# Weight blocks of the first attention split by two GpSimd transfers each, and its keys as split products

## The chip, the cores and the metric

The kernel runs on one core of a Trainium2 chip. The metric is the device time of one execution in microseconds (us). Its engines run side by side, each through its own list of instructions in order: TensorE (PE in the profile; its weight loads are PEld), VectorE (DVE), ScalarE (ACT), GpSimd (POOL) and SyncE (SP, which here only issues transfers). An instruction whose input isn't ready holds up all that stand behind it on its engine.

## The reference

Two transformer blocks follow each other on 256 tokens of width 1024, in fp32. The change lies in the first block's attention:

```python
u = rms_norm(h, pre_mix_gain[l])
proj = u @ w_in[l]
qa, ka, va, qb, kb, vb, g = jnp.split(proj, SPLITS, axis=-1)
qa = rope(...); ka = rope(...); qb = rope(...); kb = rope(...)
o_swa = windowed_gqa_sink_attention(qa, ka, va, attn_sink[l], pos, is_real)
o_diff = differential_attention(qb, kb, vb, lam, lambda_init, diff_subln_gain[l], is_key)
gates = jax.nn.sigmoid(g + b_gate[l])
```

`h` is the tokens behind 16 meta tokens, 272 columns that count. `o_swa` has 16 query and 4 key heads of 64, `o_diff` 8 heads that each subtract one softmax from another. Everything after it (branch products, output product, a gated feed-forward, and the whole second block) is as before in both kernels.

## The kernel before

All activations lie transposed, features on the partitions, tokens along the row. A weight matrix is stored in blocks of 128 output columns: one block is a 128x1024 fp32 tile (512 KB), which holds 8 squares of 128x128, one for each 128 input features.

A product of a block with the activations is made in one of two ways. `gemm_whole` (line 341) multiplies the fp32 block with fp32 activations, 8 products. `gemm` (line 325) works on numbers that are split into a high part of type fp32r and a low part, the remainder: high weight x high activation, high weight x low activation, low weight x high activation, 24 products, the 16 with the high weights first. The activations are split once (`uh`, `ul`), the weights block by block in `load_w`: SP loads the block into one of three `raw` buffers (line 299), ScalarE writes the high part `wh` as a copy in fp32r (line 309), VectorE the low part `wl = raw - wh` (line 311); `wh` and `wl` have three buffers each. (`wshare` is 0 throughout, so that the subtraction is always VectorE's.)

The first attention's projections are 52 blocks: 8 for the queries (`w_qb`), 8 for the keys (`w_kb`) and 8 for the values (`w_vb`) of the differential heads, 8 for the queries of the windowed heads (`w_qa`), 4 for their keys and values (`w_kva`), 16 for the gates (`w_gate1`). The 8 of `w_kb` and the first 2 of `w_kva`, the keys, go through `gemm_whole`; the other 42 through `gemm`. The first two blocks of all, one of keys and one of values, are loaded ahead of everything (`wfirst`). The keys and queries are then rotated (`rope`): ScalarE copies the product out of PSUM, VectorE shuffles it, GpSimd multiplies and adds (lines 511 to 513), and ScalarE and VectorE split the result.

Sixteen attention units (one differential head, or two windowed heads) stand in the order `ORDER`; the projections of a unit are written two units ahead of its attention, the gates' blocks between the units. A scheduler turns this into one list per engine; the lists are fixed when the program is built. Behind the units come 8 blocks of the differential branch (`branch_d`, `w_bd`), and from there on every block is split in the same way.

## Time and profile before

| | us |
|---|---|
| three timed runs, median (lowest to highest) | 992.06 (989.26 to 992.2) |
| the profiled execution's own time | 991.08 |
| its span, first to last instruction | 988.8 |

| engine | busy us | share of the span |
|---|---|---|
| TensorE, products | 967.2 | 98% |
| TensorE, weight loads | 902.1 | 91% |
| VectorE | 686.8 | 69% |
| ScalarE | 545.3 | 55% |
| GpSimd | 223.4 | 23% |

The shares are over the whole program; the first attention is its first quarter, so its own shares have to be asked for by the stretch. Products of TensorE are pipelined: the duration of one overlaps the next, and how long a run of them takes is read from their starts. An fp32 product appears as two instructions in the trace, a split one as one.

### The profile page before, as it was taken

Reading aid. Unit: us, or ns where it says so; the run is one execution under the profiler, and the core shown is the slowest. Engines: PE = TensorE matmul, PEld = TensorE weight load, DVE = VectorE, ACT = ScalarE, POOL = GpSimd, SP = SyncE. Lnnn points to the kernel's source line nnn. Section 1 sums busy time; section 2 is a strip of 40 time slices with the busy share of each in tenths; the row PEclk is TensorE's granted clock in tenths of the full one; section 3 lists DMA queues with packets and bytes.
Section 4 is the critical chain, followed back from the end, with each engine's and each line's share of the span. In section 5 each row is a group of like instructions: output and inputs, shape, how many; then the busy total and the mean of one; then the engine's idle time right before and its main releaser. Section 6 shows DMA issues by size and latency. Waiting matters only on the chain.

```text
span 988.8 us, 18641 instructions
## 1 busy us (share of the span) xinstructions
PE 967.2 (98%) x7218; PEld 902.1 (91%) x7218; DVE 686.8 (69%) x1466; ACT 545.3 (55%) x1097; POOL 223.4 (23%) x258
## 2 busy tenths in 40 slices
PE   9999999999999999999999899999999999999996
PEld 8888998998988989999999788887799999999885
DVE  6788789888655777666554639967687686666544
ACT  5566566667554756555545344335666565555443
POOL 5534326232240123121100312121021102222002
PEclk9999999999999999999999899999999999999999
DMA  6433333332436566555675242333045255555551
GB/s 231 164 110 105 124 113 128 105 120 96 152 124 193 171 209 195 193 195 192 215 212 187 86 132 83 129 107 107 1 164 188 97 191 190 195 192 193 192 192 64
DMA packets 42023, 149.26 MB, mean 151 GB/s; under 512 B 4728, under 2 KB 5376, under 8 KB 41808
## 3 DMA queue, kind: packets, MB, share of 16 engines
q1 hardware_dynamic: 40896, 145.47, 44.4%
q0 software_dynamic: 608, 2.03, 0.7%
q8 instruction: 56, 0.92, 0.4%
q10 hardware_dynamic: 432, 0.59, 0.2%
q14 instruction: 31, 0.25, 0.1%
HBM read 147.01 MB, written 1.06 MB: 150 GB/s over the span
## 4 chain that ended last, share of the span: by engine, by line
PE 56%; DVE 8%; ACT 2%; issue 1%; DMA 0%; ACTq 0%; DVEq 0%
PE mm L325 36%; PE mm L341 4%; PE s L325 2%; PE ac L1651 2%; PE ac L1650 2%; PE ac L1647 2%; DVE fg L868 1%; DVE wl L311 1%; PE mm L1410 1%; PE mm L820 1%; PE mm L818 1%; PE mm L819 1%; DVE ul L292 1%; DVE y L1011 1%; DMA raw<-w_xq 0%
## 5 line engine op out<-in xcount | busy, mean ns | idle before, releaser
L309 ACT ACTIVATE wh<-raw 128x1024 fp32r<-128x1024 f32 (+1 forms) x232 | 243.6, 1052 | 199.7 <-PE mm L325 115.7
L311 DVE TENSOR_TENSOR wl<-raw,wh 128x1024 fp32r<-128x1024 f32 (+1 forms) x232 | 286.9, 1238 | 94.1 <-ACT wh L309 89.6
L325 PE MATMUL mm<-uh,wh 128*128 128x256 f32 (+1 forms) x1040 | 253.1, 282 | 0.0
L325 PE MATMUL mm<-ul,wh 128*128 128x256 f32 (+1 forms) x1040 | 251.2, 281 | 0.2 <-DVE ul L292 0.2
L325 PEld LDWEIGHTS mm<-uh,wh 128*128 128x128 f32 x1040 | 195.5, 188 | 2.9 <-issue 1.4
L325 PEld LDWEIGHTS mm<-ul,wh 128*128 128x128 f32 x1040 | 195.7, 188 | 0.8 <-DVE ul L292 0.4
L325 PE MATMUL mm<-uh,wl 128*128 128x256 f32 (+1 forms) x1040 | 148.6, 281 | 0.0
L325 PEld LDWEIGHTS mm<-uh,wl 128*128 128x128 f32 x1040 | 131.9, 188 | 0.5 <-issue 0.2
L341 PE MATMUL mm<-u,raw 128*128 128x256 f32 (+1 forms) x464 | 109.7, 387 | 0.0
L894 POOL TENSOR_TENSOR sg<-sg,rs 128x256 f32<-128x256 f32 x44 | 49.6, 1129 | 223.4 <-ACT sg L893 182.1
L341 PEld LDWEIGHTS mm<-u,raw 128*128 128x128 f32 x464 | 85.5, 190 | 14.3 <-issue 1.1
L898 DVE TENSOR_TENSOR ft<-mm,sg 128x256 f32<-128x256 f32 x42 | 17.8, 424 | 46.5 <-PE mm L325 44.7
L325 PE MATMUL mm<-f_h,wh 128*128 128x256 f32 x176 | 41.1, 276 | 0.0
L325 PE MATMUL mm<-f_l,wh 128*128 128x256 f32 x176 | 41.1, 276 | 0.0
L1650 PE MATMUL ac<-wh,f_l 128*128 128x512 f32 (+1 forms) x110 | 38.0, 346 | 0.0
L1651 PE MATMUL ac<-wl,f_h 128*128 128x512 f32 (+1 forms) x110 | 37.8, 347 | 0.0
L1647 PE MATMUL ac<-wh,f_h 128*128 128x512 f32 (+1 forms) x110 | 37.8, 343 | 0.0
L892 DVE TENSOR_TENSOR sg<-mm,rs 128x256 f32<-128x256 f32 x40 | 17.0, 424 | 26.1 <-PE mm L325 26.1
L325 PEld LDWEIGHTS mm<-f_h,wh 128*128 128x128 f32 x176 | 33.0, 188 | 0.0
L325 PEld LDWEIGHTS mm<-f_l,wh 128*128 128x128 f32 x176 | 33.0, 188 | 0.0
L511 POOL TENSOR_TENSOR ropem<-rawq,cqt 128x256 f32<-128x256 f32 x16 | 18.4, 1152 | 59.9 <-ACT rawq L508 59.8
L341 PE MATMUL mm<-os,raw 128*128 128x256 f32 x128 | 28.2, 380 | 0.0
(545 smaller groups left out, 2090.9 us busy)
## 6 DMA issues: line engine op xcount, KB each, us to landing
raw<-w_gu SPq DMA_DIRECT2D x88, 512.0 KB, 4.3
raw<-w_dn SPq DMA_DIRECT2D x22, 512.0 KB, 3.5
raw<-w_pr SPq DMA_DIRECT2D x20, 512.0 KB, 3.5
raw<-w_gate SPq DMA_DIRECT2D x16, 512.0 KB, 3.5
raw<-w_out SPq DMA_DIRECT2D x16, 512.0 KB, 3.7
raw<-w_fo SPq DMA_DIRECT2D x16, 512.0 KB, 3.7
raw<-w_kb SPq DMA_DIRECT2D x8, 512.0 KB, 3.5
raw<-w_vb SPq DMA_DIRECT2D x8, 512.0 KB, 3.5
```

The source lines that it names most:

```text
L292: dve.scalar_tensor_tensor(l, src, gain, h.bitcast(F32), OP.mult, OP.subtract)
L309: act.activation(h[:, :kt * c], raw[:, :kt * c], AF.Copy)
L311: eng.tensor_tensor(l[:, :kt * c], raw[:, :kt * c], h[:, :kt * c].bitcast(F32), OP.subtract)
L325: pe.matmul(o, w[:, k * P:(k + 1) * P], xs[k][i], start=(first and n_ == 0), stop=(last and n_ == len(steps) - 1))
L341: pe.matmul(o, raw[:, k * P:(k + 1) * P], x, start=(k == 0), stop=(k == len(xs) - 1))
L511: pool.tensor_tensor(m[:, :n], raw[:, :n], c, OP.mult)
L892: dve.tensor_tensor(sg, o, rs, OP.mult)
L894: pool.tensor_tensor(sg, sg, rs, OP.mult)
L898: dve.tensor_tensor(t, o, sg, OP.mult)
L1647: m = pe.matmul(o, f_h[:, k, tok], h[:, cols], start=(k == 0), stop=False)
L1650: pe.matmul(o, f_l[:, k, tok], h[:, cols], start=False, stop=False)
L1651: pe.matmul(o, f_h[:, k, tok], l[:, cols], start=False, stop=(k == FT - 1))
```

## The change

For 50 of the 52 blocks (all but the two that are loaded ahead) `load_w` uses no `raw` buffer. GpSimd issues a transfer from the weights in HBM straight into `wh`, which converts to fp32r on the way; ScalarE writes `-wh` into `wl`; GpSimd issues a second transfer of the same weights that adds them to what is in `wl`. So `wl` holds the weights less `wh`, as before. The blocks of the keys are no longer multiplied in fp32 but go through `gemm` like the others. From `branch_d` on, `load_w` is what it was.

```diff
         def load_w(src, kt, c=P, raw=None, tag=""):
 
+            h = wpool.tile([P, KT * P], F32R, name="wh", tag="wh" + tag, bufs=3)
+            l = wpool.tile([P, KT * P], F32R, name="wl", tag="wl" + tag, bufs=3)
+            h_, l_ = h[:, :kt * c], l[:, :kt * c]
+            if dma[0] and raw is None:
+                pool.dma_start(h_, src)
+                act.activation(l_, h_.bitcast(F32), AF.Copy, scale=-1.0)
+                pool.dma_start(l_, src, accum_op=OP.add)
+                return h, l
             if raw is None:
                 raw = raw_w(src, kt)
-            h = wpool.tile([P, KT * P], F32R, name="wh", tag="wh" + tag, bufs=3)
-            l = wpool.tile([P, KT * P], F32R, name="wl", tag="wl" + tag, bufs=3)
-            wcount[0] += 1
-            act.activation(h[:, :kt * c], raw[:, :kt * c], AF.Copy)
-            eng = pool if wshare[0] and wcount[0] % wshare[0] == 0 else dve
-            eng.tensor_tensor(l[:, :kt * c], raw[:, :kt * c], h[:, :kt * c].bitcast(F32), OP.subtract)
+            act.activation(h_, raw[:, :kt * c], AF.Copy)
+            dve.tensor_tensor(l_, raw[:, :kt * c], h_.bitcast(F32), OP.subtract)
             return h, l
...
         us_v = [(uh[:, k, :], ul[:, k, :]) for k in range(KT)]
-        us_k = [u[:, k, :] for k in range(KT)]
         ist.close()
+        dma[0] = True
...
         def keys_b(h):
             kb[h] = key_tiles("kb", 3)
-            gemm_whole(d["w_kb"][h], us_k, NK, lambda o: key(o, *kb[h], dve), ps=bank(),
+            gemm(d["w_kb"][h], us_v, NK, lambda o: key(o, *kb[h], dve), ps=bank(),
                  raw=wfirst.pop(0) if wfirst else None)
...
             for p in range(2):
-                gemm_whole(d["w_kva"][p], us_k, NK, lambda o, p=p: key(o, *ka[p], pool))
+                gemm(d["w_kva"][p], us_v, NK, lambda o, p=p: key(o, *ka[p], pool))
...
         def branch_d(j):
+            dma[0] = False
             gemm(d["w_bd"][j], ods, NT, lambda o: act.activation(bd[:, j, :], o, AF.Copy))
```

On GpSimd, where the input's squares end and the rotations begin, there stood before (s0 are the squares, ropem, kraw and qraw the rotations; numbers tell buffers apart):

```order
L457 TENSOR_TENSOR s0_152<-hT_71 128x272
L457 TENSOR_TENSOR s0_156<-hT_71 128x272 [waits DMAHW6_49]
L511 TENSOR_TENSOR ropem_263<-rawq_260,ckt_189 128x272 [waits DVE_49,Activation_49]
L511 TENSOR_TENSOR ropem_350<-rawq_347,cqt_193 128x256 [waits DVE_49,Activation_49]
L513 TENSOR_TENSOR kraw_258<-ropem_263,rot_259 128x272 [waits DVE_49,Pool_49]
```

In the same place of the changed kernel:

```order
L461 TENSOR_TENSOR s0_152<-hT_71 128x272
L308 DMA wh_335<-w_qb 128x1024
L461 TENSOR_TENSOR s0_156<-hT_71 128x272 [waits DMAHW7_49,PE_49]
L308 DMA wh_377<-w_kb 128x1024 [waits PE_49]
L308 DMA wh_421<-w_vb 128x1024 [waits DVE_49,PE_49]
L310 DMA wl_336<-w_qb 128x1024 [waits Activation_49]
L515 TENSOR_TENSOR ropem_283<-rawq_280,ckt_189 128x272 [waits DVE_49]
L308 DMA wh_464<-w_qb 128x1024 [waits DMASW0_49,PE_49]
L517 TENSOR_TENSOR kraw_278<-ropem_283,rot_279 128x272 [waits DVE_49,Pool_49]
L310 DMA wl_378<-w_kb 128x1024 [waits Activation_49]
L308 DMA wh_587<-w_qa 128x1024 [waits DMASW1_49,PE_49]
L310 DMA wl_422<-w_vb 128x1024 [waits Activation_49]
```

The transfers stand between the rotations: the one into a block's `wh` waits for TensorE, which frees the buffer, the one into its `wl` for ScalarE, and another block's `wh` mostly stands between the two.

On ScalarE, behind the chain of the norm (rs_a), there stood before (wh the conversions, rawq the copies out of PSUM, kb_h and vb_h parts of keys and values):

```order
L362 ACTIVATE rs_a_163<-rs_a_163 128x272 [waits Activation_49]
L309 ACTIVATE wh_385<-raw_383 128x1024 [waits DMAHW5_49,PE_49]
L309 ACTIVATE wh_429<-raw_427 128x1024 [waits DMAHW6_49,DVE_49,PE_49]
L508 ACTIVATE rawq_347<-s_314 128x256 [waits PE_49,Pool_49]
L288 ACTIVATE kb_h_247<-kraw_258 128x272 [waits Pool_49]
L309 ACTIVATE wh_553<-raw_551 128x1024 [waits DMAHW7_49]
```

and now:

```order
L366 ACTIVATE rs_a_163<-rs_a_163 128x272 [waits Activation_49]
L512 ACTIVATE rawq_280<-s_249 128x272 [waits PE_49]
L309 ACTIVATE wl_336<-wh_335 128x1024 [waits DMASW0_49]
L578 ACTIVATE vb_h_289<-t_322 128x256 [waits PE_49]
L561 ACTIVATE vbm_291<-t_325 32x128 [waits PE_49]
L309 ACTIVATE wl_378<-wh_377 128x1024 [waits DMASW1_49,DVE_49]
L562 ACTIVATE vbm_291<-t_325 32x128
L309 ACTIVATE wl_422<-wh_421 128x1024 [waits DMASW2_49]
L288 ACTIVATE kb_h_247<-kraw_278 128x272 [waits Pool_49]
```

The conversions, which waited for an SP transfer, have become negations, which wait for a GpSimd transfer, at the head of the same list.

On TensorE a stretch of the middle of the stage reads, after the change (mm are the accumulators; wl_1736 ends one block, wh_1778 begins the next, t are transposes of attention):

```order
L329 MATMUL mm_1740<-ul_98,wh_1735 128x272
L329 MATMUL mm_1740<-uh_97,wl_1736 128x272 [waits DMASW4_49]
L329 MATMUL mm_1740<-uh_97,wl_1736 128x272 x3
L598 MATMUL t_1646<-base_72,pr2_222 32x128 [waits DVE_49,Activation_49]
L607 MATMUL t_1655<-base_72,pr2_222 128x128 [waits Activation_49]
L329 MATMUL mm_1740<-uh_97,wl_1736 128x272 x4
L329 MATMUL mm_1783<-uh_97,wh_1778 128x256 [waits DMASW3_49,Activation_49]
L329 MATMUL mm_1783<-ul_98,wh_1778 128x256
```

Both the first high and the first low product of a block wait for a GpSimd transfer there (DMASW).

## Rows read from the trace of the kernel before

**Rows 1.** The page: busy us by engine, and TensorE in 40 slices.
```profile
PE 967.2 (98%) x7218; PEld 902.1 (91%) x7218; DVE 686.8 (69%) x1466; ACT 545.3 (55%) x1097; POOL 223.4 (23%) x258
...
PE   9999999999999999999999899999999999999996
```

**Rows 2.** Windows: length; busy PE, PEld, DVE, ACT, POOL; clock, DMA share, GB/s.
```profile
17.70:246.30 228.60, 228.06 (x1661) 204.70 (x1661) 189.63 (x441) 144.85 (x371) 88.64 (x105) 1.00 0.36 119
```

**Rows 3.** Waits of TensorE, 17.7 to 246.3 us: total us, times, longest.
```profile
PE o L616 <- DVE pl L607: 0.5, 1, 0.5
```

**Rows 4.** Timeline of TensorE from 19 us: start, us, instruction.
```profile
19.66 3.83 PE L341 MATMUL mm<-u,raw 128*128 128x272 f32 x16
23.33 0.27 PE L568 MATMUL t<-base,vT 128*128 128x128 f32 x1
...
23.90 0.29 PE L325 MATMUL mm<-uh,wh 128*128 128x272 f32 x1
...
25.66 1.17 PE L325 MATMUL mm<-uh,wl 128*128 128x272 f32 x8
26.66 0.28 PE L325 MATMUL mm<-uh,wh 128*128 128x256 f32 x1
```

**Rows 5.** Timeline of TensorE from 198 us, behind an fp32 product.
```profile
198.20 0.49 PE L325 MATMUL mm<-uh,wh 128*128 128x272 f32 x1
198.53 0.29 PE L325 MATMUL mm<-ul,wh 128*128 128x272 f32 x1
198.66 0.29 PE L325 MATMUL mm<-uh,wh 128*128 128x272 f32 x1
```

**Rows 6.** Groups by form, 17.7 to 246.3 us: busy us, mean ns, idle.
```profile
L311 DVE TENSOR_TENSOR wl<-raw,wh 128x1024 fp32r<-128x1024 f32 x42 | 55.6, 1323 | 9.2 <-ACT wh L309 6.7 <-ACT sq L646 1.9 <-PE mm L325 0.5
L309 ACT ACTIVATE wh<-raw 128x1024 fp32r<-128x1024 f32 x43 | 45.5, 1059 | 23.2 <-PE mm L325 6.8 <-issue 4.1 <-DMA raw<-w_vb 3.6
...
L511 POOL TENSOR_TENSOR ropem<-rawq,cqt 128x256 f32<-128x256 f32 x16 | 18.4, 1152 | 59.9 <-ACT rawq L508 59.8
...
L698 DVE TENSOR_SCALAR pr<-pr,r 128x272 f32<-128x272 f32 x30 | 12.2, 447 | 0.3
...
L511 POOL TENSOR_TENSOR ropem<-rawq,ckt 128x272 f32<-128x272 f32 x10 | 8.7, 868 | 33.6 <-ACT rawq L508 26.2 <-DVE ckt L476 7.4
```

**Rows 7.** DMA view: issues, KB each, median us from issue to landing.
```profile
raw<-w_kb SPq DMA_DIRECT2D x8, 512.0 KB, 3.5
...
bt<-scr POOLq DMA_DIRECT2D x1, 1024.0 KB, 7.4
...
base<-const_b POOLq DMA_DIRECT2D x1, 384.0 KB, 6.3
base<-w_uk POOLq DMA_DIRECT2D x1, 256.0 KB, 6.2
...
base<-rel_bias POOLq DMA_DIRECT2D x1, 1.0 KB, 6.0
scr<-rtab POOLq DMA_DIRECT2D x1, 12.0 KB, 3.4
```

**Rows 8.** Line 408, GpSimd's seven transfers: ns of an issue, and landing.
```profile
L408 POOL DMA_DIRECT2D base<-const_b x1: 734/734/734, 349.1 to 349.1; - x1
...
L408 POOL DMA_DIRECT2D cc<-const_c x1: 518/518/518, 351.4 to 351.4; - x1
...
L408 POOL DMA_DIRECT2D bt<-scr x1: 953/953/953, 480.2 to 480.2; - x1
...
DMA to landing us min/median/max: 3.4/6.2/7.4
```

**Rows 9.** DMA view, GpSimd's queue: packets, MB, share of 16 engines.
```profile
q0 software_dynamic: 608, 2.03, 0.7%
```

**Rows 10.** Timeline of TensorE: low products, third and seventh block.
```profile
18.72 1.10 PE L325 MATMUL s<-uh,wl 128*128 128x256 f32 x8
...
33.22 1.10 PE L325 MATMUL mm<-uh,wl 128*128 128x256 f32 x8
```

More of the change, by code (lines that the diff above doesn't have):

```diff
@@ L293, in split @@
             return m
-        wcount, wshare, last_w = [0], [0], [None]
+        last_w, dma = [None], [False]
         def raw_w(src, n):
@@ L765, in _program @@
             gate_of(j)
-        wshare[0] = 0
         first = [None]
```

## The prediction, made blind

> **What bounds the kernel now.** Read first the page's busy shares: TensorE is busy 98% of the span, in every slice of it [rows 1]. A busy TensorE can still be one that stands at a wait, so the second view is the stage that the change touches: from 17.7 us (the third weight block is under way) to 246.3 us (the last gate block ends), 228.6 us for 50 weight blocks, 4.57 us a block, attention between them included. There TensorE is busy 228.06 of 228.6 us, VectorE 189.6 (83%), ScalarE 144.9 (63%), GpSimd 88.6 (39%), the DMA engines 36% [rows 2]. The third view settles it: in all that stage the waits view of TensorE has one row, 0.5 us behind VectorE [rows 3]. So the stage is as long as TensorE's own work. What VectorE, ScalarE or GpSimd are given or spared counts only if TensorE comes to wait for it, or stops having to do something.
>
> **The change, part by part.**
>
> *Keys as split products.* A key block before is eight fp32 products, each of which the trace shows as two matmul instructions: 16 of them from 19.66 to 23.33 us, 3.67 us [rows 4]. A split block of the same 272 columns is 24 instructions at 0.126 us: 23.90 to 25.66 us is 14 of them, and the eight low products 1.00 us [rows 4], so 24 x 0.126 = 3.02 us. Each key block saves 0.65 us of TensorE time. Also, a split product that follows an fp32 one costs more: 0.33 us to the next start where 0.13 is usual [rows 5], 0.2 us, about once a block. In the stage nine key blocks are affected (seven of the differential heads, two of the windowed ones; the very first stands before 17.7 us): 9 x (0.65 + 0.2) = 7.7 us less. That is a gain on the path, since TensorE is the path.
>
> *VectorE's subtractions go, ScalarE's copies become negations.* 42 subtractions of 1.32 us, 55.6 us of VectorE, leave the stage; ScalarE had 43 conversions of 1.06 us and has 50 negations of the same 128x1024 shape [rows 6], +7 us on an engine at 63%. By rows 3 the first is worth nothing to TensorE by itself. The second costs nothing while ScalarE has its 84 idle us; what it costs when a negation has to stand and wait is a rival below.
>
> *The transfers.* Before, SP fills three raw buffers far ahead and a block lands 3.5 us after its issue [rows 7]; three pairs of wh and wl stand behind them. Now 50 blocks have no raw buffer: 100 issues on GpSimd, each 0.52 to 0.95 us of it in the trace [rows 8], 52 to 95 us more on an engine that has 140 idle. In GpSimd's order the high part of block n stands behind TensorE's use of block n-3 (three wh buffers), and the low part behind ScalarE's negation, which itself waits for the high part to land. So there is a chain across four blocks, from the end of the high products of block n-3 to the end of the high products of block n+1: high transfer, negation, low transfer, low products of n, high products of n+1. Its price, term by term:
> - High transfer, 512 KB: bounds 3.4 us (12 KB) and 7.4 us (1024 KB), the median of the seven GpSimd transfers 6.2, and 256 and 384 KB took 6.2 and 6.3 [rows 7, 8]. I take 6.2, the nearest sizes.
> - Negation: 1.06 us [rows 6].
> - Low transfer: no accumulating transfer is in the trace. It reads 512 KB of weights and 512 KB of what lies in SBUF, so the nearest row is the 1024 KB one, 7.4 us; lower bound 4.9 us (3.4 plus 128 packets over 16 engines at 0.18 us, as queue 0's 608 packets took 0.7% of 16 x 988.8 us, 0.18 us each [rows 9], 1.5 us), upper bound 10 us, if it pays for bytes read twice and written once (7.4 plus another 512 KB, 2 to 3 us by the difference of 3.4 and 7.4).
> - Low products 1.0, high products 2.0 us [rows 4].
> - Queues: one GpSimd issue (0.55) stands ahead of the low one, and ScalarE works on something else when the high part lands, about half an operation (0.5): 1.1 us.
> Sum: 6.2 + 1.06 + 7.4 + 1.0 + 2.0 + 1.1 = 18.8 us; with the bounds 13.5 (3.4 for the high part, 4.9 for the low) to 22.6 (7.4 and 10).
>
> Against it stands TensorE's own work over four blocks: (228.6 - 7.7) / 50 x 4 = 17.7 us. The chain is 1.1 us longer, 50/4 = 12.5 times: +14 us of TensorE waiting. Where the blocks are densest, at the start, it is worse: from 18.7 us (high products of the third block done) to 33.2 us (those of the seventh) are 14.5 us [rows 10], 4.3 short once, of which 1.1 is counted: +3. The order gives no slack there: the low products of a block stand directly ahead of the next block's high ones, so TensorE cannot go on with those.
>
> *The start.* The first key block now needs its ScalarE conversion (1.06 us) ahead of the first products. But TensorE also waits there for the input, which both kernels load in the same way; I take 0, bounds -0.5 (eight fp32 products fewer) to +1.1.
>
> *DMA engines.* The stage's transfers, nearly all of them these blocks, keep the DMA engines busy 36% of the time [rows 2]. Reading each block twice makes that 72%, and 108% if the accumulation's read of SBUF counts as much as a block. I take the 72% and no cost beyond the latencies above; the 10 us of the low transfer's upper bound stand for the other case.
>
> The sum: the profiled execution took 991.1 us (span 988.8 and 2.3 around it), 1.0 below the median of the three timed runs, 992.06. 991.1 - 7.7 + 14 + 3 = 1000.4; against the median, 1001. I say 1001 us.
>
> One rule of the Trainium skill speaks against the change. In the trace GpSimd's rope product of 256 columns takes 1152 ns and that of 272 only 868 [rows 6], so something holds GpSimd up now and then. "SBUF — State Buffer", section "SBUF: two separate sides", says that GpSimd cannot write its transfers' descriptors while VectorE runs an operation that takes both ports, and that such a transfer waits until that operation ends. If VectorE's scalings of probabilities, 30 of 447 ns in the stage [rows 6], were such operations and each transfer met one, the chain would grow by 2 x 0.45 us and the sum by 12.5 x 0.9 = 11 us, to 1012. The trace neither shows nor excludes it: its five GpSimd issues in a row took 0.52 to 0.73 us [rows 8].
>
> **The rivals.**
>
> *All transfers hidden, faster.* If high and low transfer together take no more than 10.5 us (say 4.9 and 5.5), the chain is 15.7 us, under the 17.7 of TensorE's work; only the start is short, by 1 us. Then 991.1 - 7.7 + 1 = 984 us, 985 against the median. For it: the raw transfers of the same 512 KB land in 3.5 us, 12 KB from GpSimd in 3.4, and the five rows of some 6 us are of transfers issued in one go, each behind the others [rows 7, 8]. Against it: 1 KB in 6.0 us, so that the latency is not the bytes' [rows 7]. The Trainium skill, "DMA: Bandwidth & Descriptors", section "Anatomy of one DMA — SWDGE (gpsimd) path", gives a transfer from GpSimd as 2.0 us plus its bytes over 436 GB/s, an estimate of 3.2 us for 512 KB; the trace disagrees, 6.2 us for 256 KB.
>
> *ScalarE stands at its negations, much slower.* The negation of a block waits for a landing at the head of ScalarE's queue, and the exponentials and conversions of attention wait behind it. ScalarE's idle time, 228.6 - 144.9 - 7 = 77 us, is 1.5 us a block. From a wait of 1.5 us a block on, ScalarE becomes the bound; at 2.5 us it adds 50 x 1.0 = 50 us: 991 - 7.7 + 50 = 1033. For it: a landing time of 6.2 against 3.5. Against it: the high transfer is issued up to three blocks, 13 us, ahead.
>
> *Cancelling.* A chain of 17.9 to 18.2 us gives +2.5 to +6 by its excess over 17.7, and the start's +3, against -7.7: 990 to 994 against the median, no change to be told.
>
> **How the numbers follow.** The forecast, slower by a chain slightly longer than TensorE's work: 0.42, its own range 996 to 1016 (chain 18.4 to 20.0). Hidden: 0.30. ScalarE or a far slower accumulation: 0.14. Cancelling: 0.14. A measurement of this kernel tells 0.3%, 3 us, from no change. Faster is the hidden case, 0.30, and slower the first and third, 0.56, which leaves 0.14. The range that holds 8 in 10 goes from 984 to 1025: it leaves out the slow end of the ScalarE case and the fastest hidden ones.
>
> **What would show it.** Right: in the stage after the change TensorE waits of 1 to 3 us released by the landing of wl, the greatest between 19 and 45 us; no fp32 products of u; the low transfer at 7 to 8 us to landing; the stage some 10 us longer than 228.6, and everything after it as long as before. Wrong: low transfers that land in 5.5 us or less and a TensorE without waits (hidden); or waits of TensorE on ScalarE's exponentials and of ScalarE on wh's landing (the second rival).

## The result, and the profile after

The changed kernel took 1026.13 us (median of four timed runs, 1023.66 to 1028.06) against 991.62 us for the kernel before on the same chip (989.26 to 992.2): ratio 1.0345, 95% interval 1.0324 to 1.0365. It is slower, as forecast, but by 34.5 us where 9 were forecast; 1001 us was predicted, and the range ended at 1025.

The profiled execution took 1027.67 us, its span is 1025.9 us. The page gives the busy time of each engine, then TensorE, its granted clock and the DMA engines in 40 slices, then GpSimd's DMA queue (packets, MB, share of the 16 engines' span):

```profile
PE 976.1 (95%) x7298; PEld 910.2 (89%) x7298; DVE 661.4 (64%) x1426; ACT 547.9 (53%) x1107; POOL 285.3 (28%) x358
...
PE   8899988999999999999999899999999999999996
...
PEclk9899999799999999999999989999999999999998
DMA  8999998699643646656576432334025445556641
...
q0 software_dynamic: 15008, 54.46, 23.4%
```

Against [rows 1], TensorE has gaps in the first slices, and its clock is down to 8 tenths in the second of them and to 7 in the eighth. GpSimd's queue carries 15008 packets instead of 608 [rows 9]; a packet took 23.4% x 16 x 1025.9 / 15008 = 0.26 us on the mean, where it was 0.18.

The stage ends with the first product of `w_bd`, at 246.3 us before and at 281.6 us now: 35.3 us later. What follows takes 742.5 us of the span before and 744.3 now. So nearly all of it is in the stage. The windows view of the stage, and of two pieces of it (columns as in [rows 2]):

```profile
17.70:281.60 263.90, 240.06 (x1744) 217.00 (x1743) 161.77 (x397) 150.23 (x378) 147.19 (x203) 0.95 0.89 200
29.20:36.00 6.80, 5.57 (x25) 5.58 (x26) 1.49 (x4) 1.65 (x3) 3.83 (x5) 0.50 1.09 278
179.40:193.00 13.60, 11.99 (x50) 11.04 (x51) 8.79 (x19) 6.15 (x15) 5.38 (x9) 0.50 0.67 151
```

TensorE is busy 240 of 264 us, where it was busy 228 of 229. The granted clock was 1.00 in all of the stage before; now it is 0.50, 1.2 instead of 2.4 GHz, in three stretches: these two and 3.4 us from 237.5. The DMA engines went from 36% to 89%.

The waits view of TensorE from 12 to 282 us (total us, times, longest), which had one row of 0.5 us in the stage before [rows 3]:

```profile
PE mm L329 <- DMA wl<-w_gate: 5.6, 6, 1.4
PE t L598 <- DVE pr L702: 5.0, 3, 2.5
PE mm L329 <- DMA wl<-w_kb: 4.3, 3, 2.6
PE mm L329 <- DMA wl<-w_qb: 2.1, 3, 1.4
PE mm L329 <- DMA wl<-w_qa: 1.9, 2, 1.2
PE s L540 <- DVE vbm L563: 1.7, 1, 1.7
PE mm L329 <- DMA wl<-w_vb: 1.2, 1, 1.2
PE mm L329 <- DMA wh<-w_kb: 0.8, 1, 0.8
PE s L329 <- DMA wl<-w_qb: 0.6, 1, 0.6
PE s L540 <- ACT pr L635: 0.3, 1, 0.3
...
```

Two kinds stand here: products of weights that wait for the landing of a low part (six rows of `wl`, 15.7 us together), and products of attention (t, s) that wait for VectorE or, once, for ScalarE. ScalarE and GpSimd show where the time is spent upstream:

```profile
ACT wl L309 <- DMA wh<-w_gate: 21.0, 11, 4.5
ACT wl L309 <- DMA wh<-w_kb: 10.5, 5, 3.0
...
POOL wl L310 <- ACT wl L309: 46.4, 20, 7.2
```

ScalarE stands at its negation until the high part lands (six such rows, 59.9 us in 31 waits), and GpSimd stands at the issue of the low part until ScalarE has negated. The DMA view gives the landings (columns as in [rows 7]):

```profile
wh<-w_gate POOLq DMA_DIRECT2D x16, 512.0 KB, 5.7
wl<-w_gate POOLq DMA_DIRECT2D x16, 512.0 KB, 7.2
wh<-w_qb POOLq DMA_DIRECT2D x8, 512.0 KB, 6.5
wl<-w_qb POOLq DMA_DIRECT2D x8, 512.0 KB, 6.7
```

One block of values can be followed through the chain, in the timelines of GpSimd, ScalarE, GpSimd and TensorE:

```profile
58.80 0.83 POOL L308 DMA_DIRECT2D wh<-w_vb  x1
...
66.68 1.06 ACT L309 ACTIVATE wl<-wh 128x1024 fp32r<-128x1024 f32 x1 [1.69 <-DMA wh<-w_vb]
...
68.04 0.90 POOL L310 DMA_DIRECT2D wl<-w_vb  x1 [2.10 <-ACT rawq L512]
...
73.77 1.27 PE L329 MATMUL mm<-uh,wl 128*128 128x272 f32 x8 [1.23 <-DMA wl<-w_vb]
```

The high transfer goes out 0.3 us after TensorE has let go of the buffer (58.5), lands at 66.6, is negated at once, the low one goes out at 68.0 and lands at 73.7; TensorE has waited 1.23 us by then.

**Where the 35.3 us are.** I compared every gap between the starts of two products in the stage with the usual gap of the same pair of forms in the kernel before. TensorE's own work is 3.3 us less. Gaps more than 0.3 us above the usual, outside the half-clock stretches, are counted as waits: 16 ahead of low products, 18.4 us; 2 ahead of high products, 1.5; 5 ahead of attention's products, 7.6 (0.7 before). The half-clock stretches cost 9.9 us beyond the usual, and small gaps 1.7 more. -3.3 + 18.4 + 1.5 + 6.9 + 9.9 + 1.7 = 35.1. (The waits view counts from the end of a product, so its sums are smaller: 15.7 and 7.0 us.) The same count for the experiments is in the table at the end of the next section.

**Behind attention's waits.** Followed back over 8 us through what released what, four of the five (1.3, 1.8, 1.4 and 2.7 us) come behind VectorE instructions that took 2.5 to 4.3 us more than usual, while GpSimd ran products. The longest, in the timelines of GpSimd, VectorE and TensorE:

```profile
177.85 1.01 POOL L658 TENSOR_TENSOR ms<-ms,rr 128x256 f32<-128x256 f32 x1
178.54 1.00 POOL L662 TENSOR_TENSOR osb<-osb,rr 128x256 f32<-128x256 f32 x1
...
177.49 3.47 DVE L702 TENSOR_SCALAR pr<-pr,r 128x272 f32<-128x272 f32 x2
...
181.01 0.39 PE L598 MATMUL t<-base,pr 128*32 128x128 f32 x1 [2.52 <-DVE pr L702]
```

The two scalings took 3.47 us together; in the stage before, one took 0.36 us at the median and 0.90 at most. Behind the waits of 1.3 and 1.8 us there is, further back, also a negation that stood at a landing; behind the fifth wait, of 0.4 us, there is only that.

### The profile page after: what moved, and what is told of

The parts are those of the page before. It is cut to its first block, busy times and chain, and to the rows that moved or that the text cites. A ratio compares the mean times of both kernels' runs of the same rounds, so it can differ in the third digit from the quotient of the medians.

```text
span 1025.9 us, 18869 instructions
## 1 busy us (share of the span) xinstructions
PE 976.1 (95%) x7298; PEld 910.2 (89%) x7298; DVE 661.4 (64%) x1426; ACT 547.9 (53%) x1107; POOL 285.3 (28%) x358
## 3 DMA queue, kind: packets, MB, share of 16 engines
q1 hardware_dynamic: 33696, 119.25, 35.1%
q0 software_dynamic: 15008, 54.46, 23.4%
HBM read 173.23 MB, written 1.06 MB: 170 GB/s over the span
## 4 chain that ended last, share of the span: by engine, by line
PE 58%; DVE 7%; ACT 1%; issue 1%; ACTq 0%; DVEq 0%
PE mm L329 36%; PE mm L345 5%; PE s L329 3%; PE ac L1655 2%; PE ac L1654 2%; PE ac L1651 2%; DVE fg L872 1%; PE mm L1414 1%; DVE wl L315 1%; PE mm L824 1%; PE mm L822 1%; PE mm L823 1%; DVE base L1159 0%; DVE y L1014 0%; PE s L1292 0%
## 5 line engine op out<-in xcount | busy, mean ns | idle before, releaser
L315 DVE TENSOR_TENSOR wl<-raw,wh 128x1024 fp32r<-128x1024 f32 (+1 forms) x192 | 233.7, 1219 | 81.8 <-ACT wh L314 78.2
L329 PE MATMUL mm<-uh,wh 128*128 128x256 f32 (+1 forms) x1112 | 275.8, 286 | 0.9 <-DMA wh<-w_kb 0.8
L329 PE MATMUL mm<-ul,wh 128*128 128x256 f32 (+1 forms) x1112 | 274.2, 284 | 0.0
L314 ACT ACTIVATE wh<-raw 128x1024 fp32r<-128x1024 f32 (+1 forms) x192 | 200.2, 1047 | 131.2 <-PE mm L329 73.7
L329 PEld LDWEIGHTS mm<-uh,wh 128*128 128x128 f32 x1112 | 212.4, 191 | 3.8 <-DMA wh<-w_kb 1.0
L309 ACT ACTIVATE wl<-wh 128x1024 fp32r<-128x1024 f32 x50 | 52.9, 1059 | 69.2 <-DMA wh<-w_gate 21.0
L345 PE MATMUL mm<-u,raw 128*128 128x256 f32 x320 | 73.1, 382 | 0.0
L345 PEld LDWEIGHTS mm<-u,raw 128*128 128x128 f32 x320 | 59.5, 190 | 9.3 <-DVE y L1014 0.4
L288 ACT ACTIVATE f_h<-ft 128x256 fp32r<-128x256 f32 x44 | 18.3, 419 | 35.9 <-DVE ft L902 35.8
L897 ACT ACTIVATE sg<-sg 128x256 f32<-128x256 f32 x44 | 18.1, 418 | 31.1 <-DVE sg L896 31.1
```

Source lines behind the costliest of these rows:

```text
L288: m = act.activation(h, src, AF.Copy)
L309: act.activation(l_, h_.bitcast(F32), AF.Copy, scale=-1.0)
L314: act.activation(h_, raw[:, :kt * c], AF.Copy)
L315: dve.tensor_tensor(l_, raw[:, :kt * c], h_.bitcast(F32), OP.subtract)
L329: pe.matmul(o, w[:, k * P:(k + 1) * P], xs[k][i], start=(first and n_ == 0), stop=(last and n_ == len(steps) - 1))
L345: pe.matmul(o, raw[:, k * P:(k + 1) * P], x, start=(k == 0), stop=(k == len(xs) - 1))
```

## The experiments

Theories at the start: **chain** (a block's high transfer, negation and low transfer follow each other, through three buffers and GpSimd's order, and take longer than TensorE's work of that time); **DMA engines** (89% busy: two readings of each block, one of them slower, are simply too much). Later a third came: **standing** (an engine that waits for a landing holds up attention's work behind it). A fourth, **slow VectorE** (GpSimd's products hold it up, and attention with it), is what the timeline just above shows; 9 and 13 bear on it, though they were made for other questions. The end of the stage (246.3 us before, 281.6 after) is given beside each time; it and the waits are read from one profiled execution of each kernel.

**1. The keys alone.** Edit on the kernel before, at both key calls:

```diff
-            gemm_whole(d["w_kb"][h], us_k, NK, ...
+            gemm(d["w_kb"][h], us_v, NK, ...
```

> The kernel before, with one part of the change alone: the nine key blocks become split products (converted by ScalarE, subtracted by VectorE from the raw buffer), no GpSimd transfers. By the prediction's term TensorE has 7.7 us less to do in the stage to 246 us, VectorE 9 x 1.32 = 12 us more (202 of 228 us) and ScalarE 9.5 us more, both with room: 984 us, ratio 0.992. Rival: the trace after the change shows only 3 to 6 us less TensorE work between its waits, and VectorE at 88% comes late now and then: 987 to 992 us, ratio 0.996 to 1.000.

Measured: 986.83 us against 991.69, ratio 0.9955 (0.9941 to 0.9970); end of the stage 242.0, no wait of TensorE in it, VectorE busy 200.41 of 224.30 us. So the keys are worth 4.3 us of the stage and some 4.5 of the whole, less than the 7.7 of the prediction, and VectorE's extra load costs nothing. The timeline of TensorE, behind attention's fp32 transposes, shows why a part of the 7.7 wasn't there:

```profile
24.68 0.27 PE L571 MATMUL t<-base,vT 128*32 128x128 f32 x1
24.71 0.37 PE L325 MATMUL mm<-ul,wh 128*128 128x272 f32 x1
24.92 0.29 PE L325 MATMUL mm<-uh,wh 128*128 128x272 f32 x1
25.05 0.29 PE L325 MATMUL mm<-ul,wh 128*128 128x272 f32 x1
```

The products keep their 0.125 us. The first split product starts 0.03 us behind the transpose and the next one 0.21 later: 0.24 us for two starts, as usual, so this change of kind costs nothing. In the stage before, only three split products stand directly behind an fp32 product of a key block, as in [rows 5]; there the two starts take 0.03 + 0.33 us, 0.1 more than usual. So the term of 9 x 0.2 was some 3 x 0.1. 9 x 0.65 = 5.9 without it is nearer; the rest of the difference stays open.

**2. Four `wh` buffers** instead of three in the changed kernel:

```diff
-            h = wpool.tile([P, KT * P], F32R, name="wh", tag="wh" + tag, bufs=3)
+            h = wpool.tile([P, KT * P], F32R, name="wh", tag="wh" + tag, bufs=4)
```

> The changed kernel with four wh buffers instead of three, so that in GpSimd's order the high transfers stand one block further ahead of the low ones. Same transfers, same bytes. Theory serial chain (a high transfer, a negation and a low transfer follow each other through GpSimd's queue and the buffers; the transfers themselves have room): the high part has landed long before its negation is due, and of the 35 us of the stage most go: 990 to 1005 us. Theory DMA engines (a block costs the engines nearly what TensorE needs for it, since the accumulating row takes 330 ns and the other 174): the same bytes in the same time, 1018 to 1028 us. Theory of the chain through the three wl buffers (its low transfer, not its high one, waits for a buffer): little change either, 1015 to 1026.

Measured: 1012.74 us, ratio 1.0210 (1.0188 to 1.0232); stage 263.5. Between the theories: 18 of the 35 us went. The waits for low parts fell from 18.4 to 5.4 us, as the chain says, but attention's waits did not (9.5 us), and 5.9 us of half clock are left. One of attention's waits, in the timelines of ScalarE and TensorE, has no slow VectorE instruction behind it:

```profile
224.88 1.06 ACT L309 ACTIVATE wl<-wh 128x1024 fp32r<-128x1024 f32 x1 [3.48 <-DMA wh<-w_gate]
...
227.67 0.39 PE L540 MATMUL s<-kb_h,qh 64*128 64x272 f32 x1 [2.04 <-ACT pr L635]
```

ScalarE stands 3.48 us at a negation, an exponential (pr) stands behind it, and TensorE waits for that.

**3. A negation that waits for nothing:** it reads `u` instead of `wh`, so that the low transfer doesn't stand behind the high one.

```diff
-                act.activation(l_, h_.bitcast(F32), AF.Copy, scale=-1.0)
+                act.activation(l_, other[0][:, :kt * c], AF.Copy, scale=-1.0)
```

> The changed kernel, whose negation reads another tile of the same shape (the normalised input u) instead of the high part that has just landed; the low parts are then not the residues, so the products are of other numbers, all else as before. The low transfer no longer stands behind the high one's landing, and the bytes, the accumulation and the number of instructions stay. Theory serial chain: the chain loses its high transfer of 6.2 us, TensorE hardly waits, 985 to 995 us. Theory DMA engines: 1015 to 1028 us, and the landings grow, since both transfers of a block are issued at once.

Measured: 995.44 us, ratio 1.0042 (1.0024 to 1.0060); stage 247.8. Its window (columns as in [rows 2]):

```profile
17.70:247.80 230.10, 225.06 (x1745) 206.70 (x1744) 155.26 (x403) 153.00 (x382) 146.55 (x202) 1.00 0.96 230
```

The same bytes, accumulated as before, went through in 230.1 us, with the DMA engines at 96%, and TensorE was busy 225 of them. That settles the DMA engines: they can carry the change to within 5.8 us of the keys alone (242.0). What costs is that one step waits for the landing of another. (ScalarE stands at no landing here either, so this run doesn't tell the chain from the standing.)

**4. A low transfer that doesn't accumulate:**

```diff
-                pool.dma_start(l_, src, accum_op=OP.add)
+                pool.dma_start(l_, src)
```

> The changed kernel, whose low transfer overwrites wl instead of adding to it (the low part is then the whole weight block in the narrower type). Order, waits and buffers stay; only the work of the transfer falls, by the rows of the high one from 330 to 174 ns each: the DMA engines have 2.8 us a block to do instead of 4.1. Theory DMA engines: the stage loses nearly all its waits, 985 to 995 us. Theory serial chain: the low transfer's landing falls from 6.9 to some 6.2 us, and as the part of the chain that binds (high transfer, negation, issue of the low one, next high issue) does not hold the low landing, 1010 to 1024 us.

Measured: 1000.62 us, ratio 1.0093 (1.0073 to 1.0113), between the two expectations; stage 248.8. (What follows the stage took 752.7 us in the profiled execution, 10 more than before; why wasn't looked into.) Window, queue and landings:

```profile
17.70:248.80 231.10, 225.58 (x1745) 207.53 (x1744) 155.50 (x402) 154.07 (x384) 131.97 (x206) 1.00 0.75 230
```

```profile
q0 software_dynamic: 15008, 54.46, 17.6%
...
wh<-w_gate POOLq DMA_DIRECT2D x16, 512.0 KB, 4.2
wl<-w_gate POOLq DMA_DIRECT2D x16, 512.0 KB, 4.5
```

Both landings became shorter, the high one too, which was left as it was: 4.2 for 5.7, 4.5 for 7.2. So 4 us of the chain's 13 us of transfers come with the accumulation, which lengthens the transfers beside it too. With 3's result: the DMA engines don't bound the stage, but they lengthen the chain.

**5. The keys undone** (fp32 from raw buffers again, 41 blocks in two transfers):

```diff
-                gemm(d["w_kva"][p], us_v, NK, lambda o, p=p: key(o, *ka[p], pool))
+                gemm_whole(d["w_kva"][p], us_k, NK, lambda o, p=p: key(o, *ka[p], pool))
```

> The changed kernel with the keys undone: the nine key blocks of the stage are fp32 products from the raw buffers again, 41 blocks come in two GpSimd transfers. In the order there is one key block in four or five, without a transfer of GpSimd. Theory serial chain: each key block gives the chain 4.6 us of TensorE work to catch up, and most of the 27 us of waits go, against 5 us more TensorE work: 1000 to 1010 us. Theory that the chain is that of the four blocks only (the prediction's, 1.1 us a four): 41 blocks, 10 fours x 1.1 + 3, and 4.9 us back: 1003 us by the prediction, but 1025 or more if the waits do not depend on the key blocks.

Measured: 1017.29 us, ratio 1.0245 (1.0215 to 1.0276); stage 268.9. All three numbers were off. The waits for low parts went to 5.0 us, as the chain says of a loop with a fifth block in it; but attention waits 10.4 us now.

**6. Every second block by transfer:**

```diff
-            if dma[0] and raw is None:
+            nth[0] += 1
+            if dma[0] and raw is None and nth[0] % 2:
```

> The changed kernel in which every second block of the stage comes in two GpSimd transfers (23 or 25 blocks) and the others are converted and subtracted from a raw buffer as before; keys as split products. Theory serial chain: a block by transfer has about 9 us of TensorE work to arrive in, more than the two-block loop wants, so TensorE hardly waits: 985 to 990 us, as the kernel with the keys alone (986.8). Theory DMA engines: 25 x 1.4 us of load less, nothing left to wait for, the same. Rival: a negation that waits for its landing at the head of ScalarE's queue now holds up the conversion of the other blocks too: 992 to 1000 us.

Measured: 1007.24 us, ratio 1.0157 (1.0139 to 1.0175); stage 258.8. Missed. Half the transfers, landings of 5.5 and 5.8 us, and TensorE still waits 8.3 us for low parts and 5.2 in attention. The buffers are shared with the other blocks, so a transferred block still gets its buffer only three blocks ahead; fewer transfers didn't make that longer.

**7. Only the high part by transfer,** the low one subtracted by VectorE from a raw buffer:

```diff
-                act.activation(l_, h_.bitcast(F32), AF.Copy, scale=-1.0)
-                pool.dma_start(l_, src, accum_op=OP.add)
+                raw = raw_w(src, kt)
+                dve.tensor_tensor(l_, raw[:, :kt * c], h_.bitcast(F32), OP.subtract)
```

> The changed kernel with only the high part by a GpSimd transfer; the low part is VectorE's subtraction from a raw buffer that SyncE fills, so there is no negation and no accumulating transfer. (Six buffers of a later stage are... one buffer of a later stage is single instead of double, so the end of the stage in the trace is compared, not the whole time: 246.3 us before, 281.6 after, 242.0 with the keys alone.) Theory serial chain: GpSimd waits for no landing, the high transfers run three blocks ahead, stage end 242 to 245 us. If a landing of 6 us by itself were the trouble (three buffers are too few for it): 255 us or later.

Measured: stage 260.0 (1004.27 us). Missed, and the most telling miss: no second transfer, no chain, and 18 us later than the keys alone. Waits for weights are 2.5 us, those of attention 9.5. One of them in the timelines of GpSimd, VectorE and TensorE:

```profile
104.39 1.66 POOL L517 TENSOR_TENSOR qraw<-ropem,rot 128x256 f32<-128x256 f32 x1
105.98 0.59 POOL L308 DMA_DIRECT2D wh<-w_vb  x1
...
112.32 1.23 DVE L310 TENSOR_TENSOR wl<-raw,wh 128x1024 fp32r<-128x1024 f32 x1 [5.37 <-DMA wh<-w_vb]
...
114.14 0.36 PE L620 MATMUL o<-ph,vb_h 128*128 128x256 f32 x1 [3.10 <-DVE pm L563]
```

The transfer stands behind a rope product in GpSimd's list, lands 6.3 us later, VectorE stands 5.37 us at its subtraction, the masks and low parts of attention stand behind that, and TensorE waits 3.10 us for one of them, not for the weights. This is the third theory. By the count of starts this wait is 3.3 of the 9.5 us; behind each of the other seven there are VectorE instructions that took 1.0 to 3.3 us more than usual, so standing isn't the only thing that makes attention late.

**8. The negation on VectorE:**

```diff
-                act.activation(l_, h_.bitcast(F32), AF.Copy, scale=-1.0)
+                dve.tensor_scalar(l_, h_.bitcast(F32), -1.0, None, OP.mult)
```

> The changed kernel with the negation on VectorE instead of ScalarE. (Buffers of a later stage are single instead of double to make room, so the end of the stage in the trace is compared, not the whole time: 246.3 us before, 281.6 after.) VectorE is idle 37% of the stage after the change, ScalarE's negation started up to some us after the landing, the low issue typically 1.4 to 2 us after it. Theory serial chain, with ScalarE's own queue as a part of it: the loop of two blocks becomes 0.5 to 1 us shorter, the stage ends 10 to 25 us earlier, 257 to 272 us. Theory that only transfers count: no change, 279 to 284 us. Rival: VectorE stands at the landing and holds up the softmax work, 285 us or later.

Measured: stage 270.3 (1000.64 us; with six buffers of the second block single, its later part is 14 us shorter for reasons outside this study, so the time isn't compared; 16 was tried for that). Within the theory's range, but not by its reason: waits for low parts fell to 7.2 us, attention's rose to 15.7. VectorE, not ScalarE, now stands at landings (26 us), with the softmax behind it.

**9. GpSimd with hardly anything but transfers** (rope and head normalisation on VectorE):

```diff
-            pool.tensor_tensor(m[:, :n], raw[:, :n], c, OP.mult)
+            dve.tensor_tensor(m[:, :n], raw[:, :n], c, OP.mult)
```

and so for the seven other lines of the two.

> The changed kernel with the rope products and the products of the head normalisation moved from GpSimd to VectorE, so that in the stage GpSimd has hardly anything but its 100 transfers. After the change a block's chain is, in means over 47 blocks, 1.2 us from the free buffer to the issue of the high part, 6.2 to its landing, 0.5 to the negation, 1.1, 0.4 to the low issue, 6.7 to its landing, 1.2 to the low products and 3.9 to the end of the next block's high ones: 21.2 us in four blocks of 17.2 us of TensorE work. Theory: GpSimd's own work in front of the issues is about 1 us of it, and waits of attention behind GpSimd's rope go too: 10 to 18 us of the stage's 39.6 come back, 1008 to 1016 us, end of the stage 264 to 272. Rival: the latency alone is the matter, within 4 us of 1026; or VectorE becomes late with 50 us more work: slower than 1026.

Measured: 1027.26 us, ratio 1.0361 (1.0338 to 1.0383); stage 281.6. The rival by its time: GpSimd's own work in front of the issues is no part of the waits for weights. What it had done there it now stands: its wait for ScalarE's negation went from 46.4 to 92.7 us. But with no product on GpSimd, VectorE is held up no more, and attention's waits fell from 7.6 to 1.1 us, although ScalarE stood as long at landings (61.8 us, 59.9 without the edit). The waits for weights and the half clock took the gain, 35.8 us together instead of 29.8; that TensorE came later to attention's products for these also gave them time.

**10. Rope on VectorE and four `wh` buffers** (the edits of 9, rope only, and of 2).

> The changed kernel with the rope products on VectorE and four wh buffers. Theory: a loop of five blocks instead of four, 16 + 1.2 + 4.6 = 21.8 us against 21.5 us of TensorE work, and no rope in front of the issues: hardly any wait for wl is left, no half clock in the stage, end of the stage 245 to 255 us, 990 to 1000 us. Rival: what four buffers left (stage end 263.5, 9.5 us of it waits of attention) is of VectorE's and ScalarE's queues and stays: 1008 to 1015 us.

Measured: 1010.08 us, ratio 1.0205 (1.0184 to 1.0226); stage 263.2. The rival again: what four buffers leave has little to do with rope on GpSimd. VectorE's instructions lost 8 us instead of 35, but attention's waits fell from 9.5 to 7.7 only; behind 5.5 of these ScalarE stood at a landing and no VectorE instruction was slow.

**11. Only the nine key blocks by transfer:**

```diff
-            if dma[0] and raw is None:
+            if by_dma and raw is None:
```

> Only the nine key blocks come in two GpSimd transfers, all other blocks are converted and subtracted from raw buffers as before. Theory chain of four blocks: a block's transfers are issued when the block three before it is used, 13 to 15 us ahead; alone on the queues a landing takes 4.5 to 5 us, so the low part is there after 5 + 1 + 5 + 1.5 = 12.5 us and TensorE hardly waits: 985 to 990 us, as the keys alone without transfers (986.8). Rival: the negation at the head of ScalarE's queue holds up the conversions of the next blocks and TensorE waits in attention and for wh: 993 to 1003 us.

Measured: 993.08 us, ratio 1.0026 (1.0007 to 1.0045); stage 247.8, 5.8 us later than with the same keys and no transfer (the profiled execution was 2.4 us above the median of 12, which go from 989.61 to 999.94). Two waits for weights of a key block (3.1 and 1.6 us) and 3.4 us at half clock. The time is at the lower edge of the rival's range, but its waits of attention aren't there: neither expectation. Nine transferred blocks are enough to lose what the split keys bring.

**12. One raw buffer in the kernel before.**

> The kernel before with one raw buffer instead of three (in all stages of the program, so the stage to 246.3 us alone is read): no GpSimd transfer, but TensorE has to wait for every block: landing 3.5 + conversion 1.1 + subtraction 1.3 + waits of some 0.5 = 6.4 us against 4.6 us of TensorE work, 1 to 2 us a block, 80 us in the stage. It is a test of the clock: if waits of 1 to 3 us by themselves bring the granted clock down, the stage shows stretches at half the clock, as after the change; if the clock fell for the transfers' sake, it stays full, as in the stage before.

Measured: 989.67 us, stage 246.6, full clock: no test. SyncE's list came out the same as before; the blocks loaded ahead seem to hold the count at three, whatever the line says. It only repeats the time.

**13. The subtraction on GpSimd,** in the kernel before, without transfers (`wshare` from 0 to 1):

```diff
-        wcount, wshare, last_w = [0], [0], [None]
+        wcount, wshare, last_w = [0], [1], [None]
```

> The kernel before with GpSimd in place of VectorE for the subtraction of the low parts in the stage (some 35 blocks or more); no GpSimd transfer at all, nothing read twice. A product of 256 columns takes GpSimd 0.87 us, so one of 1024 some 2 to 3.5 us, and TensorE will have to wait for it now and then. It is a test of the clock without transfers: if TensorE's waits of 1 to 3 us bring the granted clock down, the stage shows stretches at 1.2 GHz after such waits; if it is the transfers (or their contention) that do it, the clock stays at 2.4 GHz whatever TensorE waits. Time: 995 to 1020 us if GpSimd is late, 992 if its slowness is hidden (then there is no test).

Measured, one run: 1000.74 us, stage 258.4. TensorE waits 13 times, 12.8 us, 1.85 us at the longest, and the clock stays full. For the clock this would speak for the transfers as the cause, but the longer waits were missing. For attention it shows something else: GpSimd is busy 177 us of the stage instead of 89, VectorE's instructions take 68 us more than usual, and attention's products wait 10.1 us, without a transfer to stand at.

**14. The negation on VectorE and four `wh` buffers** (the edits of 8 and 2).

> The changed kernel with the negation on VectorE and four wh buffers, nothing else. Both theories of the wait for a landing are tested at once: the loop of five blocks (16 us of transfers and negation and 4.6 of TensorE's against 21.5 us of work) gives TensorE time, and ScalarE stands at no landing. If the rest of e2 (9.5 us of attention's waits, 5.4 for wl, 5.9 of half clock) came from ScalarE standing at its negations: end of the stage 245 to 253 us, 990 to 997 us. If any in-order engine that stands at a landing costs the same: 258 to 268 us, 1003 to 1013 us, with waits of attention behind VectorE in place of those behind ScalarE.

Measured: 1019.33 us, ratio 1.0289 (1.0246 to 1.0333); stage 270.5, attention's waits 13.8 us. Later than either expectation. ScalarE stands at no landing, VectorE 26 us, and it is worse than 2: taking the standing off ScalarE alone brings nothing.

**15. Every subtraction twice on GpSimd** (13 with its subtraction written two times).

> As e13, with every subtraction on GpSimd done twice (the second writes what the first wrote), so that GpSimd needs 4.8 us a block and TensorE waits longer for it, still without a transfer of GpSimd's. In e13 TensorE waited 13 times, 1.85 us at most, and the clock stayed full; after the change most falls came behind a wait of 2 to 3 us. If longer waits alone bring the clock down: several waits above 2 us and stretches at half the clock in the stage. If it takes the transfers as well: such waits and a full clock. Time: 1040 to 1110 us.

Measured, one run: 1127.54 us, later than expected. No transfer of GpSimd's in the stage, and thirteen stretches at half clock, 99.0 us together, each beginning in a wait of TensorE or within 1.2 us behind one. One of them in its timeline, and the window of another:

```profile
266.59 0.39 PE L596 MATMUL t<-base,pr 128*32 128x128 f32 x2 [2.90 <-DVE pr L700]
...
268.54 0.28 PE L327 MATMUL mm<-ul,wh 128*128 128x256 f32 x1
268.66 0.28 PE L327 MATMUL mm<-uh,wh 128*128 128x256 f32 x1
...
269.16 0.42 PE L327 MATMUL mm<-ul,wh 128*128 128x256 f32 x1
269.38 0.42 PE L327 MATMUL mm<-uh,wh 128*128 128x256 f32 x1
```

```profile
166.40:176.60 10.20, 6.59 (x34) 6.02 (x33) 8.29 (x16) 5.45 (x15) 5.41 (x6) 0.50 0.30 103
```

TensorE waits 2.90 us, once more 0.66 us (to 268.08), and 2.2 us after it first began again its products come every 0.22 us instead of every 0.12. So the fall takes no transfer of GpSimd's. The 9.9 us at half clock after the change are put down to the waits on these grounds, as a price on top of them.

**16. Three single buffers of the second block** on the kernel of 1.

> The kernel of e1 (keys as split products, no transfers) with three buffers of the second block single instead of double (row, xs and xs6, as in e8). In e8, where six were single, the program behind the first attention took 729 us of the span instead of 742 to 746 in all other runs. If one of these three does it, 972 to 978 us and the end of the stage stays at 242; if it is one of the other three (et, dl, du) or the order that comes with the room, 986 to 988 us as e1, or a little slower.

Measured: 984.86 us, ratio 0.9948 (0.9932 to 0.9965), stage 242.0: the interval is that of 1 (0.9955). Not these three buffers; why the later part of 8 is shorter stays open.

| kernel | end of the stage | waits ahead of weight products | waits of attention | half clock, beyond the usual | VectorE above its usual |
|---|---|---|---|---|---|
| before | 246.3 | 0 | 0.7 | 0 | 22 |
| after | 281.6 | 19.9 | 7.6 | 9.9 | 39 |
| 1 keys alone | 242.0 | 0 | 0 | 0 | 24 |
| 2 four wh | 263.5 | 6.6 | 9.5 | 5.9 | 35 |
| 3 negation free | 247.8 | 4.2 | 2.2 | 0 | 28 |
| 4 plain low | 248.8 | 4.3 | 2.7 | 0 | 31 |
| 5 keys fp32 | 268.9 | 5.8 | 10.4 | 4.6 | 36 |
| 6 every second | 258.8 | 9.5 | 5.2 | 3.3 | 31 |
| 7 high only | 260.0 | 2.5 | 9.5 | 3.1 | 33 |
| 8 negation VectorE | 270.3 | 9.6 | 15.7 | 1.5 | 34 |
| 9 GpSimd free | 281.6 | 22.0 | 1.1 | 13.8 | 1 |
| 10 rope, four wh | 263.2 | 7.8 | 7.7 | 5.7 | 8 |
| 11 keys by transfer | 247.8 | 5.5 | 0 | 1.7 | 24 |
| 13 subtract GpSimd | 258.4 | 2.7 | 10.1 | 0 | 68 |
| 14 negation VectorE, four wh | 270.5 | 11.6 | 13.8 | 3.5 | 39 |

The last column adds up what VectorE's instructions took in the stage above the median of the same form before (forms that VectorE hadn't before aren't counted). All is in us. In 13 none of the waits ahead of weight products is for a landing, and in 14 those ahead of high products (4.5 of the 11.6 us) are released by ScalarE's exponentials.

Of the kernels that bring all 50 blocks in two transfers, only 3 and 4, which take the landing of the high part out of the chain or make both landings shorter, cure most of both kinds of waits at once, and with them the clock.

## Why the prediction was right and wrong

**The bound: right.** TensorE's work sets the stage, and everything behind the stage is as long as before (742.5 and 744.3 us).

**The keys: 7.7 us forecast, 4.3 to 4.9 measured** (experiment 1). The 0.65 us a block hold product by product; the 0.2 for the change of kind, counted nine times, is 0.1 and occurs three times. The rest, over 1 us, stays open.

**The chain across four blocks: right in kind and nearly in size.** The n-th transfers can be matched with the n-th group of 16 high and 8 low products. Means over 47 blocks:

| term | forecast | measured |
|---|---|---|
| high transfer | 6.2 | 6.23 |
| negation | 1.06 | 1.06 |
| low transfer | 7.4 | 6.66 |
| queues | 1.1 | 1.19 + 0.51 + 0.43 = 2.13 |
| low landing to the first low product | 0 | 1.22 |
| low products to the end of the next high ones | 3.0 | 3.89 |
| sum | 18.8 | 21.2 |

The sum of the right column has to be four block periods, since the loop closes (263.9 / 50 x 4 = 21.1), so it proves nothing; the terms do. The transfers were right within 0.8 us together. The forecast of its price, 14 + 3 = 17 us of waits for low parts, compares with 18.4 in the trace, and they are of 0.4 to 2.8 us and released by the landing of `wl`, as foretold. There is luck in how near the price came: the forecast has every loop 1.1 us too long, while in the trace 16 of the 50 blocks wait and a low part has landed 1.22 us ahead of its product at the mean. Experiments 2, 3 and 4, which make the loop five blocks long, take the high landing out of it, or shorten both landings, bring these waits to 5.4, 2.9 and 2.5 us: the chain is shown. What the last two rows of the table have in common was not in the forecast: TensorE's list has attention's products between the low products of a block and the high ones of the next, so the loop contains some of them.

**The step that failed: attention and the clock were priced at nothing.** The sum prices TensorE's waits for low parts and no others. Of the negations it says *"The second costs nothing while ScalarE has its 84 idle us"*, and leaves their standing to a rival; VectorE is only spared work; and a wait counts at its own length. This left out 17 of the 26 us that were missing:

- *Attention, 6.9 us more of TensorE's waits.* Two things make attention late. One is a VectorE that is held up while GpSimd runs its products; the forecast had looked at the other direction alone, GpSimd held up by VectorE. Over the stage VectorE's instructions took 39 us more than usual, 22 before; 13 of them lost over 1 us, none before; and four of the five waits, 7.2 of 7.6 us, come behind such instructions. Experiment 9 (1 us lost, 1.1 us of waits, ScalarE still standing) and 13 (68 us lost, 10.1 us of waits, no transfer) speak for it. The other is standing: idle time on the average is no cover in an in-order list; what counts is which work is behind the standing instruction when TensorE wants it. ScalarE stood 59.9 us, 1.2 us a block, under the line of 1.5 that the second rival drew. In the changed kernel one wait of 0.4 us comes of that alone; in 2, 7 and 10 waits of 2.1, 3.3 and 2.2 us do. So the rival's mechanism was there beside the forecast's, far below its price. How the 6.9 us divide between the two wasn't settled: in 10, with little lost on VectorE, 7.7 us are left.
- *The clock, 9.9 us.* In the trace three stretches at 1.2 GHz begin in or right behind waits of TensorE: one of 2.6 us at 27.8, two of 1.3 and 2.5 us from 176.7, one of 1.4 us at 235.7. Experiment 15 has them without any transfer, and the kernel before has one behind the stage, 1 us after two waits of 0.8 us (from 307.5 to 309.6), with GpSimd idle (window, columns as in [rows 2]):

```profile
310.60:313.90 3.30, 3.30 (x18) 3.30 (x17) 2.07 (x2) 2.93 (x6) 0.00 (x0) 0.50 0.61 189
```

In 3 and 4, with 4.3 us of waits ahead of weight products or less, it didn't happen in the stage. How long or how often a wait must be was not settled: 11 shows a fall behind one wait of 3.1 us, the changed kernel none behind one of 1.7 us at 168, 13 none in thirteen waits up to 1.85 us, and in 8 25.3 us of waits brought one stretch of 3.4 us.

The rest of the 26 us: 4.4 of the keys by this count (TensorE's own work fell by 3.3), 2.9 of waits for weights, 1.7 of small gaps.

**DMA engines at no cost: half right.** They don't bound the stage (experiment 3, 96% busy, no loss of that size), but their load was nearer to the 108% that the forecast set aside than to its 72%: 0.89 x 263.9 = 235 us of work, 103% of the stage before, against 0.36 x 228.6 = 82. Experiment 3 shows how little room that leaves. And the accumulating packets make all landings longer (experiment 4: 4.2 and 4.5 us for the gate blocks instead of 5.7 and 7.2). The forecast's landings came out right all the same, perhaps because the rows of [rows 7] that they were taken from are of transfers queued behind each other; that wasn't tested.

**The rule on GpSimd's descriptors,** that would have added 11 us, didn't show: the issues took 0.53 to 1.23 us, where [rows 8] has 0.52 to 0.95, and the low landings were under the forecast's 7.4 us at the mean (6.7). The other figure that was weighed, in the Trainium skill's "DMA: Bandwidth & Descriptors", section "Anatomy of one DMA — SWDGE (gpsimd) path", an estimate of 3.2 us for 512 KB, is below every one of the 100 landings of the stage; the shortest took 3.7 us, the high ones 6.2 us at the mean, and 4.2 for the gate blocks with less load.

The hidden case (0.30) was excluded by the low transfer's 6.7 us; 10.5 us for both would have been needed and it was 12.9. Experiment 4 has 8.7 for the gate blocks, under that limit, and its stage still ends 6.8 us behind the keys alone: some waits are left even then.

## What to carry to other kernels

A transfer into a buffer that also needs a step of a compute engine and a second transfer is a chain; write its length against the work of as many blocks as there are buffers, with everything that stands in between in the in-order lists, and look for every engine that waits for a landing: what stands behind it pays, however idle that engine is on the mean. Look too at what GpSimd's products do to VectorE once its list is held up by issues. Where TensorE was never idle, price its waits above their length, since its clock may fall behind them. And price the parts of a change apart: here the keys were worth 4.5 us (ratio 0.9955), and the transfers that came with them cost 39.

## What the runs showed of the hardware

After the change an instruction of VectorE on 128x2 elements took 2.84 us, while GpSimd, behind its issue at 68.04 us, ran products one after the other (timelines of GpSimd and VectorE):

```profile
68.66 1.05 POOL L515 TENSOR_TENSOR ropem<-rawq,cqt 128x256 f32<-128x256 f32 x1
69.36 1.04 POOL L661 TENSOR_TENSOR rr<-rr,ms 128x256 f32<-128x256 f32 x1
70.05 1.04 POOL L516 TENSOR_TENSOR rot<-rot,sqt 128x256 f32<-128x256 f32 x1
...
68.38 2.84 DVE L696 TENSOR_TENSOR es<-nb,nsink 128x2 f32<-128x2 f32 x1
```

The 16 such instructions of the kernel before took 0.27 us on the mean and 0.70 at most. The Trainium skill, "SBUF — State Buffer", section "Who interferes with whom", says that a VectorE instruction with two inputs in SBUF contends with a GpSimd instruction that reads SBUF, and that the pair of ports they share is an exclusive lock; the trace agrees with that, in the direction that the prediction hadn't looked at: it is VectorE that stood. Over the stage VectorE's instructions took 39 us more than their usual time, 22 before, for the same 88 us of products on GpSimd; in 9, with none, 1 us. That these products come closer together behind the issues, at which GpSimd stands, is likely the reason; no run tests it.

A packet of the accumulating transfer costs the engines more: 0.26 us a packet over the queue with 15008 packets, 17.6% x 16 x 1001.5 / 15008 = 0.19 without the accumulation.
